# RMS-norm row factors moved behind the products in a two-layer decoder trunk

## The chip, the cores and the metric

The kernel runs on one core of one Trainium2 chip. The metric is the device time of one execution, in microseconds (us). A profile of one execution, taken by the hardware profiler, shows what each engine did: TensorE (PE, with its weight loads PEld), VectorE (DVE), ScalarE (ACT), GpSimd (POOL) and SyncE (SP), which issues the DMAs.

## The reference

Two layers of a decoder trunk over 256 rows of 1024 numbers, all float32. What matters here is where the norms stand:

```
def rms_norm(x, g):
    y = x * rsqrt(mean(x * x, axis=-1) + EPS)
    return y * g

for i in range(2):
    h = rms_norm(x, attn_norm_g[i])
    x = x + mixer_i(h)                        # layer 0: attention; layer 1: gMLP + convolution
    x = x + swiglu(rms_norm(x, ffn_norm_g[i]))

def swiglu(h):  g, u = split(h @ w_in);  return (silu(g) * u) @ w_out
```

The factor `rsqrt(mean(x * x) + EPS)` is one number per row, so it commutes with a product over the columns; the gain `g` is one number per column. In layer 1 the mixer projects `h` to four parts (`gu`, `gv`, `ca`, `cg`) and adds a bias to each before a gelu or a sigmoid; `ca * sigmoid(cg)` goes through a causal convolution of 31 taps.

## The kernel before

The 256 rows are two tiles of 128 (m = 0, 1); the 1024 columns are eight blocks of 128, or two halves of 512 (n = 0, 1). `xs` holds the residual by rows in SBUF. Each float32 product is made of three passes of TensorE (`passes`, L223 to L228): operands are split into a rounded high part and the remainder. For the weights, `Block.split_hi` (L133, ScalarE) and `Block.split_lo` (L137, VectorE, for some blocks GpSimd) do that. The steps lie in a queue `todo`; `tick` and `pump` take them out as products are written down, `Block.at` takes out what a product needs at once, and `held` stops `tick`. Weights come in blocks of 1 MB (L116) into three raw buffers.

Where one stage ends and the next begins, `close` (L372 to L411) does the norm. It happens three times: **site 0** (attention to the first feed-forward), **site 1** (first feed-forward to layer 1's mixer) and **site 2** (mixer to the second feed-forward). At each:

1. The last eight steps of the output product of m = 0 (`tail_steps`) run, and `residual` (L358, VectorE) adds the result to `xs`; `square` (L302, ScalarE) sums the squares.
2. `row_factor` (L307, L308 on VectorE, a power on GpSimd at L310) makes the factor, `norm_rows` (L331, VectorE) multiplies `xs` by the factor and by the gain, which `gain_rows` (L321) has loaded as 128 equal rows.
3. `norm_T` transposes the normed rows on TensorE (L340, four 128x128 per half), and `split` (L239 on ScalarE, L240 on VectorE) writes high part and remainder into `xT`, the moving or stationary operand of the next stage.
4. For m = 0 this is laced into the eight steps of m = 1's tail (`N_T0`); for m = 1 it is laced into the first product of the next stage by `follow` (`N_T1`). `SPLITS` says how many weight steps are taken out in between.

TensorE's order is that of the program text. In `close`, VectorE and GpSimd run in text order too (`in_order`); elsewhere the scheduler chooses.

`FeedForward.first_steps` (L426 to L438) makes the first 256 columns row-wise; `rest` (L447 to L483) makes the others transposed: two sums of 128x512 per j, silu (L468), product (L470), split. In layer 1, `gv_steps` (L1017 to L1023) is row-wise; `gated` (L1091 to L1107) makes `cg` and `ca` transposed into one bank, takes the sigmoid (L1100, ScalarE) and the product (L1101, VectorE) into `cpad`. The taps of three of the four channel tiles run on VectorE (L1075, L1077, 93 in all); those of the fourth run on TensorE and are read out at L1064. Then `mean` (L1172, TensorE) starts the layer norm of the convolution, whose chain goes back and forth between the engines up to the last rows of the output product.

Of the kernel before, what the change touches and what calls it, by code (L numbers as in the profile page):

```python
# [60 lines left out]
SPLITS = ((2, 3, 7), (12, 3, 1), (7, 3, 5))  # L61
N_T0 = (5, 4, 5)
N_T1 = (10, 5, 10)
# [9 lines left out]
def trunk_kernel(ctx: ExitStack, tc: tile.TileContext, a: dict, out: bass.AP):  # L73
# [168 lines left out]
    def in_order(*engines):  # L242
# [12 lines left out]
        ("attn_g", a["attn_norm_g"][0].rearrange("(k p) -> k p", p=P)),  # L255
# [13 lines left out]
    assert nvec <= 64  # L269
    vec = consts.tile([P, 64], F32, name="vec")  # L270

    def load_vecs(names):
        vec_rows = scratch()[:64, :P]
        for name, src in vec_src:
            if name in names:
                nc.sync.dma_start(vec_rows[rows[name]:rows[name] + src.shape[0], :], src)
        return vec_rows

# [7 lines left out]
    nc.gpsimd.memset(neg_half, -0.5)  # L286
    mask = consts.tile([P, S], F32, name="mask")
# [4 lines left out]
    vec_rows = load_vecs(("attn_g",))  # L292
# [11 lines left out]
    def row_factor(ss):  # L304
# [4 lines left out]
        r = small.tile([P, 1], F32, name="rm")  # L309
        nc.gpsimd.tensor_tensor(r, t[:, 1:2], neg_half[:, :1], op=ALU.pow)  # L310
        return r

# [22 lines left out]
    def norm_T(m, n, xn, xT, ptag):  # L335

        pt = ptag()
        ms = slice(m * P, (m + 1) * P)
        for j in range(4):
            nc.tensor.transpose(pt[:, j * P:(j + 1) * P], xn[n][:, j * P:(j + 1) * P], ident)  # L340
        split(xT[0][:, 4 * n:4 * n + 4, ms], xT[1][:, 4 * n:4 * n + 4, ms], pt.rearrange("p (a b) -> p a b", b=P))
# [14 lines left out]
    def residual(m, n, pss):  # L356
        ns = slice(n * 512, (n + 1) * 512)
        nc.vector.tensor_tensor(xs[:, m, ns], pss[m][n], xs[:, m, ns], op=ALU.add)  # L358
# [13 lines left out]
    def close(site, lhs, ws, k0, pss, gB, ptag, tail0=True):  # L372
# [3 lines left out]
        ss = [small.tile([P, 2], F32, name="ss") for _ in range(MT)]  # L376

        def end(m, n):
            residual(m, n, pss)
            square(m, n, ss[m])  # L380

# [29 lines left out]
        return xT, follow  # L411


    class FeedForward:
        def __init__(self, layer, fp, ptag):
            self.layer = layer
# [9 lines left out]
        def first_steps(self, xT, m):  # L426
# [9 lines left out]
            nc.scalar.activation(sg[:, :256], ps[:, :256], AF.Silu)  # L436
# [10 lines left out]
        def rest(self, xT, extra=iter(()), cut_last=False):  # L447
# [852 lines left out]
```

## Time and profile before

| what | value |
|---|---|
| median of 3 runs | 631.66 us (630.54 to 631.96) |
| the profiled execution | 633.2 us |
| its span, first to last instruction | 631.4 us |
| mean granted clock of TensorE in it | 0.989 of full speed |
| TensorE busy | 609.0 us, 96% of the span |
| VectorE / ScalarE / GpSimd busy | 67% / 55% / 19% |
| read from HBM | 102.69 MB, 164 GB/s over the span |

How to read it: TensorE is busy almost all the time, so a microsecond is won only where TensorE waits, runs at the lower of its clock levels (1.2 instead of 2.4 GHz), or has work taken away. A row of a timeline gives start, duration, engine, line, operation and shapes, and in brackets how long the engine was idle before it and who released it. Matmul records overlap, since their ends are modelled; the time between two starts is the better measure.

### The profile page before, as it was taken

What the parts mean: (1) busy time and instruction counts of PE and PEld (TensorE: products, weight loads), DVE (VectorE), ACT (ScalarE), POOL (GpSimd) and SP (SyncE); (2) the same over time, 40 slices, a digit from 0 to 9 for tenths busy, and PEclk for the clock granted to TensorE, in tenths of its full rate; (3) what the DMA queues carried; (4) which work ended last, traced back from release to release, by engine and by line L of the source; (5) the groups of instructions that cost most, each with busy time, mean ns of one, the idle gap of its engine ahead of it and who ended that gap; (6) DMA issues with size and microseconds to landing.
All of it is one profiled execution on the core that took longest, in us unless ns stands there. A gap on an engine that the chain in (4) does not pass through costs nothing.

```text
span 631.4 us, 8906 instructions
## 1 busy us (share of the span) xinstructions
PE 609.0 (96%) x3420; PEld 517.6 (82%) x3420; DVE 421.1 (67%) x710; ACT 345.7 (55%) x621; POOL 121.7 (19%) x97
## 2 busy tenths in 40 slices
PE   7989799999999999999998999988999999999997
PEld 5867577787988888888886899867988888888886
DVE  3799998547666648664446389986766666665431
ACT  5764686555655587553446775446455555554320
POOL 1998321101000000000003695550000000000000
PEclk9999799999999999999999799999999999999999
DMA  7855424224766437555552553225656555555401
GB/s 248 308 196 175 158 106 132 70 66 149 245 225 215 146 128 266 185 168 185 199 197 67 167 199 134 68 89 178 208 193 201 196 174 173 193 199 190 145 0 67
DMA packets 72791, 104.32 MB, mean 165 GB/s; under 512 B 3068, under 2 KB 56492, under 8 KB 72748
## 3 DMA queue, kind: packets, MB, share of 16 engines
q1 hardware_dynamic: 72748, 103.74, 49.5%
q8 instruction: 27, 0.44, 0.3%
q14 instruction: 16, 0.13, 0.1%
HBM read 102.69 MB, written 1.05 MB: 164 GB/s over the span
## 4 chain that ended last, share of the span: by engine, by line
PE 52%; issue 29%; DVE 11%; POOL 3%; ACT 2%; DMA 1%; SPq 1%; POOLq 0%; DVEq 0%; ACTq 0%
PE mm L233 15%; PE mm L225 8%; PE mm L227 8%; PE mm L234 8%; PE mm L226 8%; DVE wlo L137 3%; DVE scr L331 2%; PE tq L700 1%; DMA raw<-in_even_w_in 1%; POOL rm L310 1%; DVE t L627 1%; PE po L728 1%; ACT whi L133 1%; DVE t L621 1%; PE tq L718 1%
## 5 line engine op out<-in xcount | busy, mean ns | idle before, releaser
L133 ACT ACTIVATE whi<-raw 128x1024 fp32r<-128x1024 f32 (+1 forms) x192 | 197.7, 1040 | 175.7 <-PE mm L233 80.1
L137 DVE TENSOR_TENSOR wlo<-raw,whi 128x1024 fp32r<-128x1024 f32 (+1 forms) x166 | 206.3, 1248 | 124.5 <-ACT whi L133 122.9
L233 PE MATMUL mm<-xT,whi 128*128 128x512 f32 x640 | 226.8, 399 | 0.0
L234 PE MATMUL mm<-xT,wlo 128*128 128x256 f32 x640 | 179.7, 281 | 0.0
L233 PEld LDWEIGHTS mm<-xT,whi 128*128 128x128 f32 x640 | 120.2, 188 | 29.6 <-issue 0.2
L234 PEld LDWEIGHTS mm<-xT,wlo 128*128 128x128 f32 x640 | 120.9, 189 | 0.0
L225 PE MATMUL mm<-whi,xT 128*128 128x512 f32 (+1 forms) x176 | 68.2, 387 | 0.6 <-ACT xT L545 0.5
L137 POOL TENSOR_TENSOR wlo<-raw,whi 128x1024 fp32r<-128x1024 f32 (+1 forms) x26 | 62.9, 2439 | 19.7 <-ACT whi L133 19.6
L227 PE MATMUL mm<-whi,hT_lo 128*128 128x512 f32 (+1 forms) x176 | 66.5, 378 | 0.0
L226 PE MATMUL mm<-wlo,hT_hi 128*128 128x512 f32 (+1 forms) x176 | 66.5, 378 | 0.0
L225 PE MATMUL mm<-whi,hT_hi 128*128 128x512 f32 (+1 forms) x176 | 66.4, 378 | 0.0
L227 PE MATMUL mm<-whi,xT 128*128 128x512 f32 (+1 forms) x176 | 64.1, 364 | 1.1 <-DVE xT L240 1.1
L226 PE MATMUL mm<-wlo,xT 128*128 128x512 f32 (+1 forms) x176 | 64.3, 366 | 0.5 <-DVE wlo L137 0.5
L310 POOL TENSOR_TENSOR rm<-st,neg_half 128x1 f32<-128x1 f32 x8 | 7.1, 894 | 188.9 <-DVE st L308 188.9
L225 PEld LDWEIGHTS mm<-whi,xT 128*128 128x128 f32 x176 | 34.5, 196 | 7.8 <-issue 1.6
L227 PEld LDWEIGHTS mm<-whi,xT 128*128 128x128 f32 x176 | 34.6, 196 | 6.8 <-DVE xT L240 1.8
L226 PEld LDWEIGHTS mm<-wlo,xT 128*128 128x128 f32 x176 | 34.7, 197 | 4.8 <-DVE wlo L137 1.3
L225 PEld LDWEIGHTS mm<-whi,hT_hi 128*128 128x128 f32 x176 | 33.1, 188 | 6.4
L226 PEld LDWEIGHTS mm<-wlo,hT_hi 128*128 128x128 f32 x176 | 33.1, 188 | 6.4
L227 PEld LDWEIGHTS mm<-whi,hT_lo 128*128 128x128 f32 x176 | 33.0, 188 | 6.4
L464 DVE TENSOR_TENSOR scr<-mm,scr 128x256 f32<-128x256 f32 x80 | 33.2, 418 | 5.8 <-ACT scr L463 5.7
L1077 DVE SCALAR_TENSOR_TENSOR cv<-cpad,cw,cv 128x256 f32<-128x256 f32 x87 | 35.7, 481 | 0.2
(226 smaller groups left out, 868.6 us busy)
## 6 DMA issues: line engine op xcount, KB each, us to landing
raw<-in_ffn_w_in SPq DMA_DIRECT2D x44, 1024.0 KB
raw<-in_ffn_w_out SPq DMA_DIRECT2D x22, 1024.0 KB
raw<-in_even_w_in SPq DMA_DIRECT2D x10, 1024.0 KB
raw<-in_odd_w_in SPq DMA_DIRECT2D x8, 1024.0 KB
raw<-in_even_w_out SPq DMA_DIRECT2D x4, 1024.0 KB
raw<-in_odd_w_out SPq DMA_DIRECT2D x4, 1024.0 KB
xs<-in_x SPq DMA_DIRECT2D x4, 256.0 KB
raw<-in_even_w_in SPq DMA_DIRECT2D x4, 256.0 KB
```

The costliest lines, as they stand in the source:

```text
L133: nc.scalar.activation(self.half(f)[0][:, r], self.source(f)[:, r], AF.Copy)
L137: self.lo_engine.tensor_tensor(lo[:, r], self.source(f)[:, r], hi[:, r].bitcast(F32), op=ALU.subtract)
L225: nc.tensor.matmul(ps, lhs[0], rhs[0], start=first, stop=False)
L226: nc.tensor.matmul(ps, lhs[0], rhs[1], start=False, stop=False)
L227: nc.tensor.matmul(ps, lhs[1], rhs[0], start=False, stop=last)
L233: nc.tensor.matmul(bank, w[0], x[2][:, k, :, :].rearrange("p a b -> p (a b)"), start=k == 0, stop=False)
L234: nc.tensor.matmul(bank[:, :S], w[1], x[0][:, k, :], start=False, stop=k == KT - 1)
L310: nc.gpsimd.tensor_tensor(r, t[:, 1:2], neg_half[:, :1], op=ALU.pow)
L331: nc.vector.scalar_tensor_tensor(xn[n], xs[:, m, n * 512:(n + 1) * 512], r, gB[:, n * 512:(n + 1) * 512], op0=ALU.mult, op1=ALU.mult)
L464: nc.vector.tensor_tensor(s, bank[:, :S], s, op=ALU.add)
L621: nc.vector.scalar_tensor_tensor(t1v, psv, rx[m], c, op0=ALU.mult, op1=ALU.mult)
L1077: nc.vector.scalar_tensor_tensor(conv[:, ct, :] if t == TAPS - 1 else acc, cpad[:, ct, t:t + S], cw[:, t, ct:ct + 1], acc, op0=ALU.mult, o ...
```

## The change

The row factor is no longer applied before the transposition. `close` transposes the raw residual as soon as it is added, and the gain is applied, as a column of factors, while high part and remainder are taken out of PSUM. The factor is computed later and applied behind the products: as the scale of the first silu, as a factor of the residual addition, and as a row of factors (`factor_rows`) that multiplies transposed results.

```diff
-SPLITS = ((2, 3, 7), (12, 3, 1), (7, 3, 5))
-N_T0 = (5, 4, 5)
-N_T1 = (10, 5, 10)
+N_T0 = ((1, 3), (1, 3), (1, 3))
+REST = (4, 4, 4)
+N_T1 = ((1, 4), (1, 2), (1, 4))
...
+    def factor_rows(r, ptag):
+
+        pb = ptag()
+        for m in range(MT):
+            dg = scratch()[:, :P]
+            nc.vector.tensor_scalar(dg, ident, r[m], None, op0=ALU.mult)
+            nc.tensor.matmul(pb[:, m * P:(m + 1) * P], ones, dg, start=True, stop=True)
+        rB = act.tile([P, S], F32, name="rB", tag="rB")
+        nc.scalar.activation(rB, pb[:, :S], AF.Copy)
+        return rB[:, None, :].to_broadcast([P, 2, S])
...
-    def gain_rows(src):
-        g = act.tile([P, D], F32, name="gB", tag="gB", bufs=1)
-        nc.sync.dma_start(g, bcast(src))
-        return g
-
-    def norm_rows(m, ss, gB, splits):
-
-        r = row_factor(ss)
-        pump(splits)
-        xn = []
-        for n in range(2):
-            xn.append(scratch())
-            nc.vector.scalar_tensor_tensor(xn[n], xs[:, m, n * 512:(n + 1) * 512], r, gB[:, n * 512:(n + 1) * 512],
-                                           op0=ALU.mult, op1=ALU.mult)
-        return xn
...
+    def x_T(m, n, ptag):
         pt = ptag()
+        for j in range(4):
+            nc.tensor.transpose(pt[:, j * P:(j + 1) * P], xs[:, m, (4 * n + j) * P:(4 * n + j + 1) * P], ident)
+        return pt
+
+    def x_split(m, n, pt, gain, xT, js=range(4)):
+
         ms = slice(m * P, (m + 1) * P)
...
+        for j in js:
+            nc.scalar.activation(xT[0][:, 4 * n + j, ms], pt[:, j * P:(j + 1) * P], AF.Copy, scale=col(gain, 4 * n + j))
+        for j in js:
+            k = 4 * n + j
+            nc.vector.scalar_tensor_tensor(xT[1][:, k, ms], pt[:, j * P:(j + 1) * P], col(gain, k),
+                                           xT[0][:, k, ms].bitcast(F32), op0=ALU.mult, op1=ALU.subtract)
...
+            nc.vector.scalar_tensor_tensor(xs[:, m, ns], pss[m][n], r[m], xs[:, m, ns], op0=ALU.mult, op1=ALU.add)
...
-        held[0] = True
         region = in_order("DVE", "Pool")
         end(0, 1)
-        xn0 = norm_rows(0, ss[0], gB, SPLITS[site][0])
         for i, (n, k) in enumerate(tail_steps(lhs, ws, k0, 1, pss, BY_BLOCK)):
+            if i == REST[site]:
+                held[0] = True
             if i == 3 and ws[0].index + 4 < len(plan):
                 plan[ws[0].index + 4].ahead()
-            if i == N_T0[site]:
-                norm_T(0, 0, xn0, xT, ptag)
-                pump(SPLITS[site][1])
+            if i in N_T0[site]:
+                turn(0, N_T0[site].index(i), ptag)
             if k == 3:
                 end(1, n)
-        norm_T(0, 1, xn0, xT, ptag)
-        xn1 = norm_rows(1, ss[1], gB, SPLITS[site][2])
+        rs.append(row_factor(ss[0]))
 
         def follow(steps, ptag):
 
             for i, _ in enumerate(steps):
-                if 0 <= i - N_T1[site] < 2:
-                    norm_T(1, i - N_T1[site], xn1, xT, ptag)
-            held[0] = False
+                if i in N_T1[site]:
+                    turn(1, N_T1[site].index(i), ptag)
+                    if i == N_T1[site][1]:
+                        rs.append(row_factor(ss[1]))
+                        held[0] = False
             region.close()
...
-            nc.scalar.activation(sg[:, :256], ps[:, :256], AF.Silu)
+            nc.scalar.activation(sg[:, :256], ps[:, :256], AF.Silu, scale=self.r[m])
...
+                if i == 9:
+                    rB = factor_rows(self.r, self.ptag)
...
-                sg = scratch()
-                nc.scalar.activation(sg, sums[0], AF.Silu)
+                sg = sums[0]
+                sgv = sg.rearrange("p (a b) -> p a b", b=S)
+                nc.gpsimd.tensor_tensor(sgv, sgv, rB, op=ALU.mult)
+                nc.scalar.activation(sg, sg, AF.Silu)
...
-            nc.vector.tensor_tensor(gn[:, m, :], ps, bv, op=ALU.add)
+            nc.vector.scalar_tensor_tensor(gn[:, m, :], ps, r[m], bv, op0=ALU.mult, op1=ALU.add)
...
         follow(gv_steps(0), spare)
+        rB = factor_rows(r, spare)
+
+        def scaled(ps):
+            t = scratch()
+            nc.vector.tensor_tensor(t.rearrange("p (a b) -> p a b", b=S), ps.rearrange("p (a b) -> p a b", b=S), rB, op=ALU.mult)
+            return t
...
-                    sigmoid = nc.scalar.activation(sgm, ps[:, :S], AF.Sigmoid, bias=col("b_in", 12 + ct))
-                    nc.vector.scalar_tensor_tensor(cpad[:, ct, TAPS - 1:], ps[:, S:], col("b_in", 8 + ct), sgm,
+                    t = scaled(ps)
+                    sigmoid = nc.scalar.activation(sgm, t[:, :S], AF.Sigmoid, bias=col("b_in", 12 + ct))
+                    nc.vector.scalar_tensor_tensor(cpad[:, ct, TAPS - 1:], t[:, S:], col("b_in", 8 + ct), sgm,
                                                    op0=ALU.add, op1=ALU.mult)
...
+            t = scaled(pu)
             for f in range(2):
-                gelu = nc.scalar.activation(guT[:, 2 * j + f, :], pu[:, f * S:(f + 1) * S], AF.Gelu_apprx_tanh,
+                gelu = nc.scalar.activation(guT[:, 2 * j + f, :], t[:, f * S:(f + 1) * S], AF.Gelu_apprx_tanh,
                                             bias=col("b_in", 2 * j + f))
```

The rest is bookkeeping: the four gains are loaded as columns with the other vectors (site 0's by a load and a transposition of eight rows during attention), the three loads of 512 KB by `gain_rows` go, the helpers that layer 0's start had for itself are now shared, `r` is handed on from `close`, and the tile of ones is made at the start.

## Rows read from the trace of the kernel before

**Rows 1.** Busy times by stretch, feed-forward 0: stretch, length, busy of PE, PEld, DVE, ACT, POOL, PEclk, DMA.
```profile
256.00:272.00 16.00, 16.00 (x92) 13.88 (x91) 10.43 (x16) 8.87 (x14) 0.00 (x0) 1.00 0.53 179
```

**Rows 2.** Timeline of TensorE at site 0.
```profile
146.36 0.40 PE L227 MATMUL mm<-whi,cT_lo 128*128 128x512 f32 x1
146.87 0.33 PE L340 MATMUL tq<-ident,scr 128*128 128x128 f32 x1
...
151.03 0.28 PE L226 MATMUL mm<-wlo,xT 128*128 128x256 f32 x1
151.87 0.39 PE L227 MATMUL mm<-whi,xT 128*128 128x256 f32 x1 [0.56 <-DVE xT L240]
...
154.00 0.28 PE L226 MATMUL mm<-wlo,xT 128*128 128x256 f32 x1
154.12 0.28 PE L227 MATMUL mm<-whi,xT 128*128 128x256 f32 x1
154.91 0.30 PE L340 MATMUL tq<-ident,scr 128*128 128x128 f32 x1 [0.50 <-DVE scr L331]
```

**Rows 3.** Waits at site 2 (432 to 447 us): total, times, longest.
```profile
PE tq L340 <- DVE scr L331: 0.5, 1, 0.5
PE mm L227 <- DVE xT L240: 0.5, 1, 0.5
```

**Rows 4.** Busy times by stretch, site 1 (columns as in rows 1).
```profile
333.63:340.47 6.84, 6.71 (x33) 5.04 (x32) 5.14 (x6) 4.35 (x6) 3.15 (x3) 1.00 0.28 96
...
344.88:347.80 2.92, 0.17 (x2) 0.03 (x1) 2.92 (x2) 1.47 (x6) 2.92 (x2) 0.96 0.00 0
347.80:354.38 6.58, 6.27 (x23) 5.16 (x24) 4.56 (x4) 3.93 (x12) 4.85 (x2) 0.50 0.39 111
```

**Rows 5.** Timeline of VectorE and GpSimd: sites 0 and 1, and a later norm.
```profile
146.06 1.41 DVE L331 SCALAR_TENSOR_TENSOR scr<-xs,rm,gB 128x512 f32<-128x512 f32 x2 [0.45 <-POOL rm L310]
...
336.39 3.62 DVE L331 SCALAR_TENSOR_TENSOR scr<-xs,rm,gB 128x512 f32<-128x512 f32 x2 [0.67 <-POOL rm L310]
337.06 2.40 POOL L137 TENSOR_TENSOR wlo<-raw,whi 128x1024 fp32r<-128x1024 f32 x1 [0.71 <-ACT whi L133]
...
419.06 2.41 DVE L1192 TENSOR_SCALAR scr<-ident,cvr 128x128 f32<-128x128 f32 x1 [0.66 <-POOL cvr L299]
```

**Rows 6.** Instructions of single lines: ns min/median/max, first and last start.
```profile
L545 ACT ACTIVATE xT<-tq,vec x16: 350/378/432, 5.9 to 17.2; 128x128 fp32r<-128x128 f32 x16
L548 DVE SCALAR_TENSOR_TENSOR xT<-tq,vec,xT x16: 334/340/351, 6.7 to 18.8; 128x128 fp32r<-128x128 f32 x16
L310 POOL TENSOR_TENSOR rm<-st,neg_half x8: 548/553/1469, 26.9 to 442.0; 128x1 f32<-128x1 f32 x8
L1023 DVE TENSOR_TENSOR gn<-mm,bv x2: 692/692/692, 352.9 to 370.6; 128x512 f32<-128x512 f32 x2
L1197 PE MATMUL cv<-scr,ones x4: 275/316/377, 418.1 to 422.3; 128*128 128x128 f32 x4
```

**Rows 7.** Layer 1's taps: VectorE's stretch (columns as in rows 1).
```profile
362.19:411.05 48.86, 48.17 (x378) 45.50 (x377) 45.38 (x109) 27.38 (x46) 33.31 (x24) 1.00 0.38 130
```

**Rows 8.** Timeline at both ends of that stretch, ScalarE, VectorE, TensorE.
```profile
360.38 1.28 ACT L1100 ACT_TABLE_LOAD   x1
...
362.19 0.48 DVE L1101 SCALAR_TENSOR_TENSOR cpad<-mm,vec,scr 128x256 f32<-128x256 f32 x1 [8.59 <-ACT scr L1100]
...
408.61 0.48 DVE L1064 TENSOR_SCALAR conv<-mm,vec 128x256 f32<-128x256 f32 x1 [0.67 <-PE mm L227]
410.47 0.81 PE L1172 MATMUL tq<-conv,ones 128*128 128x256 f32 x3
```

**Rows 9.** Two other stalls of TensorE: stretches (columns as in rows 1) and timeline.
```profile
63.38:67.14 3.76, 0.16 (x2) 0.00 (x1) 3.69 (x5) 1.58 (x4) 3.30 (x2) 1.00 0.58 234
67.14:74.30 7.16, 7.16 (x25) 5.61 (x26) 7.12 (x29) 5.02 (x17) 1.64 (x1) 0.54 0.39 146
...
427.20 0.50 PE L227 MATMUL mm<-whi,oT_lo 128*128 128x512 f32 x1 [1.93 <-DVE oT_lo L240]
```

More of the change, by code (lines that the diff above doesn't have):

```diff
@@ L268, in trunk_kernel, with load_vecs, vecs_T @@
     nvec = at
[L269 to L273, printed above, removed]
+    assert nvec <= P
+    vec = consts.tile([P, nvec], F32, name="vec")
+    def load_vecs(first, last, vec_rows=None):
+        vec_rows, r0 = scratch()[:, :P] if vec_rows is None else vec_rows, rows[first]
         for name, src in vec_src:
-            if name in names:
-                nc.sync.dma_start(vec_rows[rows[name]:rows[name] + src.shape[0], :], src)
-        return vec_rows
+            if rows[first] <= rows[name] <= rows[last]:
+                nc.sync.dma_start(vec_rows[rows[name] - r0:rows[name] - r0 + src.shape[0], :], src)
+        return vec_rows
+    def vecs_T(vec_rows, first, n, ptag):
+        pt = ptag()
+        nc.tensor.transpose(pt[:, :n], vec_rows[:n, :], ident[:n, :n])
+        nc.vector.tensor_copy(vec[:, rows[first]:rows[first] + n], pt[:, :n])
     def col(name, i):
@@ L370, in trunk_kernel, with close, turn @@
     BY_BLOCK = [(n, k) for k0 in (0, 2) for n in range(2) for k in (k0, k0 + 1)]
-    def close(site, lhs, ws, k0, pss, gB, ptag, tail0=True):
+    def close(site, lhs, ws, k0, pss, r, gain, ptag, tail0=True):
         xT = new_xT()
         ss = [small.tile([P, 2], F32, name="ss") for _ in range(MT)]
+        rs = []
         def end(m, n):
-            residual(m, n, pss)
+            residual(m, n, pss, r)
             square(m, n, ss[m])
+        def turn(m, n, ptag):
+            x_split(m, n, x_T(m, n, ptag), gain, xT)
         if tail0:
@@ L500, in trunk_kernel @@
         warm(WARM[0])
-        pt = tq()
-        nc.tensor.transpose(pt[:, :8], vec_rows[:8, :], ident[:8, :8])
-        nc.vector.tensor_copy(vec[:, :8], pt[:, :8])
+        vecs_T(vec_rows, "attn_g0", 8, tq)
         w_dk = [blocks["dk", h] for h in range(2)]
@@ L534, in trunk_kernel, with first_T, first_split @@
         pts = {}
-        def x_T(m, n):
-            pts[m, n] = pt = tq()
-            for j in range(4):
-                nc.tensor.transpose(pt[:, j * P:(j + 1) * P], xs[:, m, (4 * n + j) * P:(4 * n + j + 1) * P], ident)
-        def x_split(m, n, js=range(4)):
-            ms = slice(m * P, (m + 1) * P)
-            pt = pts[m, n]
-            for j in js:
-                nc.scalar.activation(xT[0][:, 4 * n + j, ms], pt[:, j * P:(j + 1) * P], AF.Copy, scale=col("attn_g", 4 * n + j))
-            for j in js:
-                k = 4 * n + j
-                nc.vector.scalar_tensor_tensor(xT[1][:, k, ms], pt[:, j * P:(j + 1) * P], col("attn_g", k),
-                                               xT[0][:, k, ms].bitcast(F32), op0=ALU.mult, op1=ALU.subtract)
+        def first_T(m, n):
+            pts[m, n] = x_T(m, n, tq)
+        def first_split(m, n, js=range(4)):
+            x_split(m, n, pts[m, n], "attn_g0", xT, js)
         ps_dk = [mm_bank() for _ in range(MT)]
@@ L912, in trunk_kernel @@
         run_units(units, filler)
-        xT, follow = close(0, cT, ws_b, 4, pss, gB, tq, tail0=False)
+        xT, r, follow = close(0, cT, ws_b, 4, pss, None, "ffn_g0", tq, tail0=False)
     mid = ExitStack()
@@ L931, in odd_setup @@
     def odd_setup(ptag):
-        vec_rows = load_vecs([n for n, _ in vec_src])
+        vec_rows = load_vecs("attn_g1", vec_src[-1][0])
         nc.sync.dma_start(bv, bcast(a["odd_b_in"][0, 512:1024]))
-        nc.gpsimd.memset(ones, 1.0)
         def load_ws(g0):
@@ L951, in odd_setup @@
         yield
-        pt = ptag()
-        nc.tensor.transpose(pt[:, :nvec], vec_rows[:nvec, :], ident[:nvec, :nvec])
-        nc.vector.tensor_copy(vec[:, 8:nvec], pt[:, 8:nvec])
+        vecs_T(vec_rows, "attn_g1", nvec - rows["attn_g1"], ptag)
         ws_T(ws0, 0)
@@ L1234, in trunk_kernel @@
         ws = [blocks["oo", k0] for k0 in (4, 6)]
-        xT, follow = close(2, cT, ws, 4, pss, gB, spare)
+        xT, r, follow = close(2, cT, ws, 4, pss, None, "ffn_g1", spare)
     mid.close()
```

61 lines of the change are left out of this document (31 added, 30 removed).

## The prediction

> **What bounds the kernel now.** I read the busy times by stretch first. In the feed-forwards TensorE is full, 16.00 of 16 us, beside a VectorE with 10.43 [rows 1]; nothing is to be won there except work taken off TensorE, and the change takes none off. So I looked for stretches in which TensorE waits or runs at its lower clock, with the list of waits, and then read the three norms in the timeline.
>
> Site 0: starts of 256-wide passes lie 0.12 us apart (154.00 to 154.12), yet 151.03 is followed by 151.87 and 154.12 by 154.91 [rows 2]: 0.72 and 0.67 lost, the first to the remainder of the second half of m = 0, the second to the normed rows of m = 1. Ahead of them 146.36 to 146.87 loses 0.28 (512-wide passes lie 0.23 apart). With a small one of 0.2 that is 1.9 us. Site 2 shows the same two waits, 0.5 each by their modelled ends [rows 3], so 0.7 each by starts as above, and the small one: 1.6.
>
> Site 1 is the dear one. The eight steps of m = 1's tail take 6.84 us [rows 4]; 24 passes at 0.226 and two groups of transpositions at 0.36 are 6.15. Then TensorE waits 2.92 us for the normed rows of m = 1, and comes back at a granted clock of 0.50 (1.2 GHz) for 6.58 us [rows 4], in which it does about 3.1 us of work. Why is the norm late? VectorE's two L331 take 1.41 us at site 0 and 3.62 us at site 1, where GpSimd starts a weight remainder of 2.40 at 337.06 [rows 5]: a VectorE instruction with both tensors in SBUF waits until GpSimd's is over. All together, site 1 loses 0.7 + 0.3 + 2.9 + 0.3 + 3.1 = 7.3 us.
>
> **The change part by part.**
>
> *Transposing the raw residual.* At each site the statistics, the power and L331 (twelve in all) leave TensorE's path. What is late next? The transpositions need only the addition, and of m = 0's two additions the later ends before step 1 of the tail, its place being step 3. For m = 1 the last addition ends some 0.9 us after the tail, and its transpositions stand two steps or more later. The split behind each grows: four 128x128 on ScalarE and four on VectorE, 0.38 and 0.34 each [rows 6], some 1.1 us a side when they overlap, instead of 0.6 and 0.7. For m = 0 half 1 it starts after step 3 and has four steps of 0.7 until the next stage begins: covered, by about 1 us; uncovered it costs 0.5 to 1 a site. So all of 1.9 + 1.6 goes: **-3.5**.
>
> *Weight steps.* `SPLITS` goes, and ticks run until step 4. Counted by hand, the first two feed-forward blocks are fully split before the tail of m = 1 ends at sites 0 and 2, and both `gv` blocks at site 1; what `REST` stops is for blocks used 5 us and more later. Nothing; bounds 0 and 1.2 (one remainder) a site.
>
> *Row of factors*, three times: two small products on TensorE. Their kind takes 0.32 a record and two records each [rows 6], overlapping, 0.23 a product by starts: 3 x 0.46 = **+1.4**, between 0.5 (one product each hidden in a wait) and 2. In the feed-forwards nine steps lie between factor and use, so nothing waits. Site 0's column of gains costs one transposition, 0.1.
>
> *Site 1 on TensorE.* Without stalls: tail until 333.63 + 6.15 = 339.8, eight steps of 0.69 and two transpositions until 346.0. Then the row of factors waits. The last transposition is done at 342.6; split by 344.3, statistics 0.4, power 0.55 [rows 6]: factor at 345.4. Right behind, in GpSimd's order, stand three weight remainders, so the small VectorE product on `ident` should do what L1192 did at 419.06, 2.41 us [rows 5]: 347.9. Queued behind that product on VectorE is only `gn`, which nobody awaits soon. TensorE waits 2.0 (bounds: 0, if GpSimd is not yet on; 4.9, if both diagonals are caught) and is done at 348.5, where it is now at 352.67 and 0.7 slow after that. **-4.7** up to here, without a drop of the clock.
>
> *Layer 1 on VectorE.* The question is whether these 4.7 last. From the first gate product at 362.19 to the last tap at 411.05 VectorE is busy 45.38 of 48.86 [rows 7], and TensorE comes to `mean` at 410.47, 0.6 before the last tap ends [rows 8]: both bound. The change adds six 128x512 multiplications out of PSUM, 0.69 each by L1023 [rows 6]. TensorE will finish the first gate at 354.5; multiplication, table load 1.28 [rows 8] and sigmoid put the product at 357, or up to 359.4 if GpSimd is on, since the product now reads two SBUF tensors. I take 358, 4.2 earlier. From there 48.86 + 5 x 0.69 (3.5) + waits of the three later gate products on GpSimd (between 0 and 2.4 each; GpSimd is on for half and more of this stretch, so the middle, 3.6) - idle time filled (0 to 3.5; VectorE now lags, so 3.0) = 411.0. Shift of the last tap: **-0.1**, bounds -4.7 and +4. So what site 1 wins, VectorE takes: 0 in place of -4.7. The row of factors there costs nothing then: +0.9 instead of +1.4.
>
> *A new stall.* TensorE would wait for L1064, which ends 2.0 before the last tap [rows 8], from 405.8 to 408.9: 3.1 us. Stalls of 2.92 [rows 4] and 3.76 [rows 9] were followed by 6.6 and 7.2 us near the lower clock; one of about 2.1 before 427.20 was not. The lower clock then falls on `mean` and the four steps behind it, beside VectorE's chain: 0 to 2.7, **+0.7** since most lies beside the chain.
>
> *Silu's factor on GpSimd*, twenty of 128x512, half a weight remainder of 2.40: 1.2 us each. It delays VectorE's SBUF work by as much per 11.5 us, which has 5.6 of 16 free [rows 1]; `hT` is needed only after the last j. Behind the waiting silu on ScalarE stand the copies that free TensorE's banks; a bank takes 2.9 us to fill and there are four. Nothing; without that cover 1.2 once per feed-forward. Factors inside residual, silu and `gn` replace an operand of instructions that are there. The loads of gain rows were on no path; on SyncE one small load of eight rows takes the place of a 512 KB one ahead of weight loads that wait for buffers anyway.
>
> Sum: -3.5 + 0.9 + 0.1 - 0.1 + 0.7 = -1.9, against the profiled execution's 633.2 (span 631.4), which is 1.5 above the median. On the median 631.66 that gives **629.8 us**; with its own bounds 628.3 to 631.5.
>
> **The rivals.**
>
> *The gain gets through.* VectorE's additions fit into its 3.5 us of idle time, the gate products meet GpSimd in gaps, and the scheduler puts taps where it waited. Then the last tap keeps up with TensorE: -3.5 + 1.5 - 4.7 = -6.7, no stall, 625.0. For it: the idle time is there. Against it: 3.5 us of multiplications fill it alone.
>
> *Slower: the gate products wait for GpSimd.* L1101 now reads PSUM and takes 0.48 [rows 8]; afterwards both its tensors lie in SBUF. If each of three meets a full remainder, 7.2 in place of 3.6, and the idle time doesn't shrink as much, 1.5 in place of 3.0, the last tap comes 5 us later, and the stall grows and brings the lower clock for certain: -1.9 + 5.0 = +3.1, 634.8; at half that surplus, about 632.3. It decides from a last tap 2 us later than now. The Trainium skill, page "GPSIMD Engine Reference", section "8. Key points", says the same of the SBUF interfaces: GpSimd shares them with VectorE, and contends with VectorE instructions of two SBUF inputs. By that rule all four gate products are exposed, 634.8 at worst; without it the sum would have 0 in place of 3.6 and come to 626.2. The trace agrees with the rule for L331.
>
> *The split becomes the wait.* If eight small instructions a half come later than the old two, sites 0 and 2 keep their stalls: -1.9 + 3.5 = +1.6, 633.3. Against it is the cover of 1 us.
>
> **How the numbers follow.** Forecast 0.47, gain gets through 0.22, gate products wait 0.21, split waits 0.10. About 0.2% (1.26 us) is what a measurement of this kernel can tell from no change. Of the forecast's 0.47, centred 0.6 beyond that bound, 0.29 is faster and 0.17 same; of the second all but 0.01 faster; of the third 0.16 slower, 0.05 same; of the fourth half and half. Faster 0.50, same 0.28, slower 0.22. The range leaves out half of the second and half of the third: 624.8 to 634.0.
>
> **What would show it.** Right: no wait on L331's successors at any site; granted clock 1.00 over 340 to 354; a wait of about 2 us for the diagonals ahead of the first gate; the gate products longer than 0.5 us; VectorE without gaps up to the last tap, at about the same distance from site 0 as now, and TensorE waiting some 3 us ahead of `mean`. Wrong: the last tap several us earlier (gain through) or later (slower), half clock at the row of factors, or waits on the small splits.

## The result: slower by 2.8%, and the profile after

The changed kernel takes 648.88 us (median of 4 runs, 646.61 to 652.45) beside 631.58 for the kernel before: ratio 1.0282, 95% interval 1.0228 to 1.0335. Forecast were 629.8 us and a range up to 634.0. The profiled execution is one of 646.61 us with a span of 644.9, 13.5 more than before.

To find where the 13.5 us come from I cut the span at one instruction that every version has, the residual addition of the second half of m = 0 at each site (its start on VectorE in the timeline). The stretches of all versions of this study, from their profiled executions, in us:

| kernel | start to site 0 | site 0 to 1 | site 1 to 2 | site 2 to end |
|---|---|---|---|---|
| before | 142.6 | 191.2 | 98.7 | 198.9 |
| after | 147.8 | 194.8 | 102.2 | 200.1 |
| e1 gain late | 141.9 | 193.3 | 102.5 | 200.1 |
| e2 hold longer | 147.7 | 191.3 | 104.4 | 196.1 |
| e3 no gu factor | 150.4 | 194.0 | 99.3 | 200.1 |
| e4 all three | 142.3 | 191.3 | 100.1 | 196.1 |
| e5 gu order | 150.7 | 194.8 | 104.2 | 198.6 |
| e6 vec 80 | 150.0 | 194.4 | 103.3 | 199.9 |
| e7 all kept | 141.9 | 191.3 | 105.3 | 196.1 |
| e8 diagonals on ScalarE | 140.0 | 191.3 | 104.9 | 196.1 |
| e9 steps run | 140.3 | 191.3 | 106.7 | 196.1 |
| e10 rows first at site 1 | 139.9 | 190.4 | 98.3 | 196.2 |
| e11 before, site 1 clear | 141.1 | 190.4 | 94.9 | 198.9 |
| e12 sites 0 and 2, site 1 clear | 141.0 | 191.3 | 94.7 | 196.1 |

After loses 5.2, 3.5, 3.5 and 1.2: all four stretches are longer, the attention too, in which the change has only one transposition of a column of gains. (The first stretch can't be read closer than some 3 us: the five versions with the changed kernel's attention lie at 147.7 to 150.7, mean 149.3, and the nine without its late load at 139.9 to 142.6, mean 141.2, which is 8.1 between the groups.) The list of waits of TensorE in the changed kernel begins with these (total us, times, longest):

```profile
PE tq L286 <- DMA ffn_rows<-in_ffn_norm_g: 10.4, 1, 10.4
PE tq L469 <- DVE scr L462: 4.5, 2, 2.3
PE cv L331 <- DVE scr L330: 2.6, 1, 2.6
PE tq L1151 <- ACT scr L1155: 2.6, 1, 2.6
PE tq L1196 <- DVE conv L1099: 2.0, 1, 2.0
```

The waits of [rows 3] and the stall of 2.92 [rows 4] are gone; there is no wait for normed rows or their split at any site. In their place stand these five; the fourth was 0.7 before, the other four are new. The first one in the timeline, of the SyncE queue and of TensorE:

```profile
27.21 0.25 SPq L693 DMA_DIRECT2D sub_rows<-in_diff_subln_g  x1
34.16 2.60 SPq L117 DMA_DIRECT2D raw<-in_even_w_in  x2
36.81 0.39 SPq L281 DMA_DIRECT2D ffn_rows<-in_ffn_norm_g  x1
...
31.81 0.39 PE L228 MATMUL mm<-whi,xT 128*128 128x512 f32 x1
42.63 0.27 PE L286 MATMUL tq<-ident,ffn_rows 8*128 8x8 f32 x1 [10.44 <-DMA ffn_rows<-in_ffn_norm_g]
```

SyncE issues in order. The load of eight rows of gains stands behind two weight loads that are not issued until 34.16, when their buffer is free. So it is issued at 36.81, and the transposition, which stands in TensorE's order ahead of the dv products, waits 10.44 us for it. Only the first 4.6 us of that are the wait for the issue (36.81). The other 5.4 us, from the end of the issue to the landing, pass while the two weight loads ahead of it move; the DMA share is 0.91 or more in each us from 36 to 41. VectorE works on meanwhile and the stall of 3.76 [rows 9] does not come again; 5.2 us are left at site 0 in this execution.

The second wait, behind site 0: the timeline of VectorE and TensorE, and busy times by stretch (columns as in rows 1, with GB/s last):

```profile
160.24 4.62 DVE L138 TENSOR_TENSOR wlo<-raw,whi 128x1024 fp32r<-128x1024 f32 x4
164.77 0.42 DVE L462 TENSOR_TENSOR scr<-mm,scr 128x256 f32<-128x256 f32 x1
...
165.25 0.44 PE L469 MATMUL tq<-ident,scr 128*128 128x128 f32 x2 [2.18 <-DVE scr L462]
...
162.00:164.00 2.00, 1.07 (x9) 0.86 (x8) 2.00 (x3) 1.69 (x3) 0.00 (x0) 1.00 0.09 17
166.00:168.00 2.00, 2.00 (x12) 2.00 (x11) 1.05 (x2) 1.17 (x2) 0.00 (x0) 0.50 1.09 359
```

Weight steps start again at step 4, as soon as the norm's last transposition is issued, and four remainders of the weights come onto VectorE ahead of the first product of gate and up (L462). It ends 165.2, TensorE waits 2.18 us for it and then works at 0.50, which is 1.2 GHz. Site 2 has the same wait of 2.3 and the same clock.

Site 1, GpSimd, VectorE and TensorE:

```profile
355.24 0.55 POOL L322 TENSOR_TENSOR rm<-st,neg_half 128x1 f32<-128x1 f32 x1 [4.30 <-DVE st L320]
355.76 9.46 POOL L138 TENSOR_TENSOR wlo<-raw,whi 128x1024 fp32r<-128x1024 f32 x4
...
356.12 2.06 DVE L330 TENSOR_SCALAR scr<-ident,rm 128x128 f32<-128x128 f32 x1
...
358.24 0.49 PE L331 MATMUL cv<-scr,ones 128*128 128x128 f32 x2 [2.60 <-DVE scr L330]
```

This is the forecast wait for the diagonal: 2.6 where 2.0 was said. The clock stays at 1.00 behind it. The gated products begin 15.9 us behind site 1's addition instead of 18.8, and the first gate product comes 26.2 behind it instead of 28.4. But the last tap ends 81.0 us behind it instead of 77.2. The odd stage, VectorE, ScalarE and TensorE, and the stretch of the taps:

```profile
368.76 0.92 DVE L1124 SCALAR_TENSOR_TENSOR cpad<-scr,vec 128x256 f32<-128x256 f32 x1 [3.48 <-ACT scr L1123]
373.78 1.65 DVE L1124 SCALAR_TENSOR_TENSOR cpad<-scr,vec 128x256 f32<-128x256 f32 x1
...
399.40 2.52 DVE L1054 TENSOR_SCALAR gn<-gn,mv__3786,gvr 128x512 f32<-128x512 f32 x1
401.84 3.22 DVE L1099 SCALAR_TENSOR_TENSOR cv<-cpad,cw,cv 128x256 f32<-128x256 f32 x8
404.98 0.68 DVE L1068 TENSOR_TENSOR scr<-mm,rB 128x512 f32<-128x512 f32 x1
...
406.61 1.28 ACT L1180 ACT_TABLE_LOAD   x1
408.52 1.12 PE L1151 MATMUL tq<-wsT,gn 128*64 128x128 f32 x8 [2.56 <-ACT scr L1155]
418.34 0.48 DVE L1086 TENSOR_SCALAR conv<-mm,vec 128x256 f32<-128x256 f32 x1 [4.46 <-PE mm L228]
...
368.76:423.52 54.76, 50.24 (x368) 46.68 (x367) 49.81 (x114) 28.01 (x46) 34.62 (x25) 0.94 0.35 116
```

The gate products take 0.92, 1.65, 0.47 and 0.82 instead of 0.48 each. The factor of the second gu product (L1068 at 404.98) stands behind a norm that runs beside GpSimd (2.52 where the same norm of m = 0 takes 0.55; the kernel before has this too, 2.51) and eight taps; behind it stand gelu, a table load and the scaling that frees the spatial products' bank, and TensorE waits 2.56 for that and then works at 0.50 over 408 to 414. VectorE in its turn waits 4.46 for TensorE's taps, with 12 of its own taps standing behind this read-out; before it was 0.67 [rows 8], with five. Against [rows 7] its busy time grows by 4.4 us and its idle time by 1.5: this one wait grows by 3.8, all other idle time shrinks by 2.3.

### The profile page after: what moved, and what is told of

Same layout as the page of the kernel before. It is cut to its first block, busy times and chain, and to the rows that moved or that the text cites. A ratio compares the mean times of both kernels' runs of the same rounds, so it can differ in the third digit from the quotient of the medians.

```text
span 644.9 us, 9078 instructions
## 1 busy us (share of the span) xinstructions
PE 610.0 (95%) x3433; PEld 520.8 (81%) x3433; DVE 422.4 (65%) x747; ACT 354.9 (55%) x660; POOL 147.1 (23%) x117
## 3 DMA queue, kind: packets, MB, share of 16 engines
HBM read 101.12 MB, written 1.05 MB: 158 GB/s over the span
## 4 chain that ended last, share of the span: by engine, by line
PE 69%; DVE 16%; POOL 5%; issue 3%; ACT 3%; DMA 2%; SPq 1%; POOLq 0%; ACTq 0%; DVEq 0%
PE mm L234 23%; PE mm L235 12%; PE mm L226 9%; PE mm L228 9%; PE mm L227 9%; DVE cv L1099 4%; DVE wlo L138 3%; POOL rsh L638 2%; PE tq L720 1%; PE po L748 1%; ACT whi L134 1%; DMA raw<-in_even_w_in 1%; DMA raw<-in_odd_w_in 1%; ACT xT L353 1%; PE tq L738 1%
## 5 line engine op out<-in xcount | busy, mean ns | idle before, releaser
L234 PE MATMUL mm<-xT,whi 128*128 128x512 f32 x640 | 224.3, 395 | 0.0
L496 POOL TENSOR_TENSOR scr<-scr,rB 128x512 f32<-128x512 f32 x20 | 26.8, 1340 | 206.6 <-DVE scr L491 176.3
L226 PEld LDWEIGHTS mm<-whi,xT 128*128 128x128 f32 x176 | 35.3, 201 | 6.7 <-issue 1.5
L228 PEld LDWEIGHTS mm<-whi,xT 128*128 128x128 f32 x176 | 35.2, 200 | 4.9
```

The lines of the kernel that those rows point to most:

```text
L226: nc.tensor.matmul(ps, lhs[0], rhs[0], start=first, stop=False)
L228: nc.tensor.matmul(ps, lhs[1], rhs[0], start=False, stop=last)
L234: nc.tensor.matmul(bank, w[0], x[2][:, k, :, :].rearrange("p a b -> p (a b)"), start=k == 0, stop=False)
L496: nc.gpsimd.tensor_tensor(sgv, sgv, rB, op=ALU.mult)
```

## The experiments

Times are medians; each ratio is to the kernel before, run on the same chip. The changed kernel's own ratio is 1.0282.

**e1.** The transposition of the column of gains is moved, nothing else:

```diff
         run(projections(("dq",)))
-        vecs_T(ffn_rows, "ffn_g0", 8, tq)
...
         run(projections(("dv",)))
+        vecs_T(ffn_rows, "ffn_g0", 8, tq)
```

> The changed kernel, with one edit: the transposition of site 0's column of gains stands behind the dv projection instead of ahead of it, so that TensorE no longer waits 10.4 us for its small load, which SyncE issues behind weight loads. Theory: the wait and the half clock behind it are what the attention stage lost (its end is 5.2 us later than before the change, since VectorE caught up with 5 us of its own backlog meanwhile), so this gives 5 us: about 643 to 645 against 648.9. Rival: VectorE bounds the attention stage anyway and the wait is cover for it: under 1.5 us.

Measured: 640.61 us, ratio 1.0152 (1.0109 to 1.0194). The wait is gone, site 0 comes after 141.9 us. That is 1.3% or some 8 us (by the two intervals some 4 either way), more than the 5.2 read at site 0 in one execution; it agrees with the 8.1 between the two groups of the table, and the stretch to site 1 is 1.5 shorter too. The wait behind site 0 is there as before, but not the lower clock behind it (see the last section).

**e2.** Weight steps stay stopped until the first product of the next stage is over:

```diff
                     if i == N_T1[site][1]:
                         rs.append(row_factor(ss[1]))
-                        held[0] = False
+            held[0] = False
             region.close()
```

> The changed kernel, with one edit: weight steps are held until the end of the first product of the next stage, as before the change, and not only until the second transposition of m = 1. Theory: the 2.2 us waits of TensorE for the first hidden half at both feed-forwards, and the half clock behind them, come from four weight remainders of 1.2 us that stand on VectorE right ahead of the product behind the silu; spread into earlier gaps they leave it alone: both waits under 0.7 us, 4 to 7 us less, 642 to 645. Rival: VectorE has that much to do there in any order, and the product stays late: under 1.5 us.

Measured: 643.11 us, ratio 1.0194 (1.0156 to 1.0232), 0.9% or 5.5 us, again with some 4 either way. The wait behind site 0 is 0.2 and behind site 2 gone; the two feed-forward stretches are 3.5 and 4.0 shorter. At site 1 the same edit does harm (+2.1): GpSimd in e2,

```profile
343.05 4.78 POOL L138 TENSOR_TENSOR wlo<-raw,whi 128x1024 fp32r<-128x1024 f32 x2 [61.91 <-ACT whi L134]
...
347.94 4.72 POOL L138 TENSOR_TENSOR wlo<-raw,whi 128x1024 fp32r<-128x1024 f32 x2
352.63 0.54 POOL L322 TENSOR_TENSOR rm<-st,neg_half 128x1 f32<-128x1 f32 x1
```

the power of m = 0 now comes behind four remainders (behind one in the changed kernel), and TensorE waits 2.7 and 1.6 us for the two diagonals. The program text up to this power is the same in both kernels: stopping the weight steps in the text did not keep the scheduler from placing remainders ahead of a norm's power.

**e3.** The row factor of gu is left out (the gated branch's factors, gn's and the feed-forwards' are kept):

```diff
-            t = scaled(pu)
             for f in range(2):
-                gelu = nc.scalar.activation(guT[:, 2 * j + f, :], t[:, f * S:(f + 1) * S], AF.Gelu_apprx_tanh,
+                gelu = nc.scalar.activation(guT[:, 2 * j + f, :], pu[:, f * S:(f + 1) * S], AF.Gelu_apprx_tanh,
```

> The changed kernel without the row factor of the gu projection (left out, with its two multiplications on VectorE). Theory (order): the second multiplication stands on VectorE behind a blocked normalisation and eight taps, so gelu, the table load behind it and the read-out of the spatial product come late, TensorE waits 2.6 us and runs at half clock, and its own taps end late, for which VectorE then waits 4.5 us: without it the last tap comes 4 to 7 us earlier, 642 to 645. Rival (amount, as the prediction had it): only the 2 x 0.7 us of VectorE's work go, 1.4 us, 647.5.

Measured: 641.73 us, ratio 1.0177 (1.013 to 1.0224): by the medians 1.05% or 6.6 us, for two instructions of 0.68. In the profiled execution the odd stretch is 2.9 us shorter, the wait of TensorE for the scaling 0.7 and the last tap 76.5 us behind site 1. With intervals of half a per cent on either ratio the difference of the medians is good to some 4.5 us: more than the rival's 1.4, and the profiled execution's 2.9 lies below the theory's 4 to 7. The size stays open.

**e4.** e1, e2 and e3 together (gu's row factor is left out here too).

> The three edits together (gu's row factor is left out). If the three causes are independent and all of them, the sum of the three gains, 13 to 19 us: 630 to 636, that is at the time before the change or a little under it. If they hide one another, clearly less than the sum.

Measured: 631.71 us, ratio 1.0029 (1.0006 to 1.0051). The three gains alone add up to 3.2%, together they are 2.5%: additive within the noise, since each gain is good to some 0.7%. e2's harm at site 1 is in the sum and in e4 alike (waits of 2.7 and 1.8 us, and half clock behind them). So the three causes hold most of the loss. But with them gone, and a piece of the work left out, the change is where the kernel before was; what it should have won is still missing.

**e5.** The order around the second gu product:

```diff
+        def tap():
+            with tc.issue_after(gu_scaled[0]) if gu_scaled[0] is not None else ExitStack():
+                tap_dve()
...
-                    tap_dve()
+                    tap()
...
+        credit[0] -= 3
+        held[0] = True
         last = project_gu(1)
+        held[0] = False
```

> The changed kernel with nothing left out; only the order around the second gu product is different: the weight steps stop while its passes are issued, three taps fewer are put on VectorE ahead of its row factor, and the taps that come later may not pass it. Theory (the 7 us that leaving gu's row factor out brought are order, not amount: the factor is held up by a GpSimd remainder and eight taps, behind it gelu, the table load, the scaling that frees the spatial products, and TensorE, which then loses its clock): the factor starts at about 403 instead of 404.98, the TensorE wait of 2.56 us on that scaling falls below 1, no half clock over 408 to 415, time 642 to 645.5. Rival (VectorE has too much to do; the two multiplications themselves are what costs): VectorE's work is the same, the last tap ends within 1 us of 423.5, time 647 to 650.

Measured: 651.32 us, ratio 1.0318 (1.0268 to 1.0368). The theory's steps are there (the factor comes as soon as its product is done, 60.5 us behind site 1 instead of 62.4; TensorE waits 0.8 for the scaling and keeps full clock over 408 to 416; the last tap ends 77.6 us behind site 1 instead of 81.0), and the time is not. VectorE behind the last tap:

```profile
423.08 4.56 DVE L138 TENSOR_TENSOR wlo<-raw,whi 128x1024 fp32r<-128x1024 f32 x2
427.56 0.68 DVE L1210 SCALAR_TENSOR_TENSOR scr<-tq,conv 128x512 f32<-128x512 f32 x1
```

The weight steps that were pushed back come out ahead of the mean's subtraction, where TensorE waits 3.9 us for it; from the last tap to site 2 it is 26.6 us instead of 21.3.

**e6.** Only the tile of per-row constants is wider, which moves every later tile by 32 bytes:

```diff
-    vec = consts.tile([P, nvec], F32, name="vec")
+    vec = consts.tile([P, 80], F32, name="vec")
```

> The changed kernel, with the tile of per-row constants 80 columns wide instead of 68: nothing else. It moves every tile behind it in SBUF up by 32 bytes, which puts the halves of the weights at the same offset within 64 bytes as before the change. In the changed kernel the 512-wide passes of the first feed-forward's output come every 0.234 us, where before they came every 0.227, and the first products of the second feed-forward every 0.347 a pair, where before it was 0.353. Theory (where tiles lie sets the pace of passes): the paces change by 1 to 3 percent in at least one of the feed-forwards, the time by between -2 and +2 us. Rival (the pace comes from the order of work or from what else reads SBUF): paces as in the changed kernel, time 647 to 650.

Measured: 648.17 us, ratio 1.0264 (1.0205 to 1.0323): as the changed kernel, and the paces are as there (last section). The theory falls.

**e7** is e1, e2 for sites 0 and 2 only, and e5, so that everything is computed; **e8** is e7 with the diagonals on ScalarE; **e9** is e7 without stopping the weight steps at gu and with `credit[0] -= 5`.

```diff
-                        held[0] = False
+                        held[0] = site != 1
+            held[0] = False
             region.close()
...
-            nc.vector.tensor_scalar(dg, ident, r[m], None, op0=ALU.mult)
+            nc.scalar.activation(dg, ident, AF.Copy, scale=r[m])
```

> The change with nothing left out, and three moves: the column of gains is transposed behind the dv products, weight steps stay stopped at sites 0 and 2 until the norm's steps are over (at site 1 as in the changed kernel), and the second gu product's factor has its place ahead of three taps and of the weight steps. Theory (three separate orderings cost the time): 630 to 634, no wait over 1 us behind site 0 or site 2, TensorE's wait for the diagonal at site 1 2 to 3 us as in the changed kernel. Rival (VectorE's amount of work sets the odd stage): 634 to 638, with the last tap some 3 us later against site 1 than in the run that leaves the gu factor out.

> As the run with the three moves, and the factors' diagonals are made by ScalarE (identity times the row factor as its scale) instead of VectorE. Theory (at site 1 the small VectorE product waits for a GpSimd remainder, 2.06 instead of 0.29 us): TensorE's wait at site 1 falls from 2.6 to about 1 us, the first gated products begin 1.5 to 2 us earlier, time 1 to 2 us below the run with the three moves. Rival (ScalarE is in other work there, twelve diagonals of the taps in a row, 3.6 us): the wait is as long, time the same or above.

> As the run with the three moves, nothing left out, but the weight steps are no longer stopped around the second gu product; five taps fewer are put ahead of its factor instead of three. Theory (in the run with the three moves the weight steps that were pushed behind the taps cost some 5 us between the last tap and site 2, 26 us there instead of 21): 632 to 635, from the last tap to the residual of site 2 about 21.5 us. Rival (that stretch is longer for another reason): 635 to 638, still 25 to 26 us.

Measured: e7 636.51 us, ratio 1.0089 (1.0063 to 1.0115); e8 635.37, 1.0071 (1.0047 to 1.0095); e9 638.47, 1.0106 (1.0076 to 1.0136). All three lie above the kernel before. e7 came out as its rival had it: 634 to 638 us, and the last tap, 79.1 us behind site 1, 2.7 later than in e3, which leaves gu's factor out; the stretch from site 1 to 2 is 105.3. In e8 TensorE's wait for the diagonal is 0.7 and the gated products begin 1.9 us earlier, as its theory said, yet the first gate product on VectorE comes no earlier (26.3 us behind site 1's addition, 26.4 in e7): it now waits 5.5 us for ScalarE's sigmoid, which stands behind a weight split that waits 3.24 us for its load. The 1.1 us between the medians of e7 and e8 are not clear of noise. In e9 the stretch behind the last tap is 22.3 us, as that theory said, but the last tap is later (84.4 behind site 1), because the norm beside GpSimd took 2.52 again and two weight remainders came ahead of the factor. Against the changed kernel's 102.2 us between sites 1 and 2, the three orders tried (e5, e7, e9) are 2.0, 3.1 and 4.5 longer: each frees the place it aims at and is charged at another. That it is the order and not the amount is therefore not shown; whether an order exists that has room for the two multiplications stays open.

**e11.** The question left was the prediction's own: does the odd stage eat whatever site 1 wins? Read again, the stall of [rows 4] belongs to m = 1's own two L331, not to the 3.62 us of [rows 5], which are m = 0's. VectorE and GpSimd in the kernel before:

```profile
344.83 5.59 DVE L331 SCALAR_TENSOR_TENSOR scr<-xs,rm,gB 128x512 f32<-128x512 f32 x2 [0.74 <-POOL rm L310]
...
344.76 7.89 POOL L137 TENSOR_TENSOR wlo<-raw,whi 128x1024 fp32r<-128x1024 f32 x3
```

The edit: the kernel before, with GpSimd's remainders ordered behind the normed rows of m = 1 at site 1:

```diff
-            step(f)
+            with tc.issue_after(barrier[0]) if barrier[0] and step == b.split_lo and b.lo_engine is nc.gpsimd else ExitStack():
+                step(f)
...
-        xn1 = norm_rows(1, ss[1], gB, SPLITS[site][2])
+        xn1 = norm_rows(1, ss[1], gB, 0 if site == 1 else SPLITS[site][2])
+        if site == 1:
+            behind = small.tile([P, 2], F32, name="st2")
+            barrier[0] = nc.gpsimd.tensor_copy(behind[:, 0:1], xn1[1][:, 511:512]).ins
+            pump(SPLITS[site][2])
```

> The kernel before, with one edit: at site 1 GpSimd's weight remainders are ordered behind a one-column copy that needs the normed rows of m = 1, so that none runs beside VectorE's two L331 there (5.59 us together, 1.41 at site 0). Theory (that is what made the stall of 2.92 us and the lower clock behind it): the stall falls below 1 us, granted clock 1.00 over the steps behind it, the gated products start 3 to 5 us earlier. Whether the end keeps it: if taps on VectorE bound the odd stage (as the prediction had it), the last tap moves less than 1 us and the time stays within 630 to 632; if not, 626 to 629.

Measured: 625.51 us, ratio 0.9914 (0.9885 to 0.9943). VectorE and TensorE at site 1, the clock behind it, and the stretch of the taps:

```profile
342.50 1.41 DVE L333 SCALAR_TENSOR_TENSOR scr<-xs,rm,gB 128x512 f32<-128x512 f32 x2 [0.74 <-POOL rm L312]
343.40 0.63 PE L342 MATMUL cv<-ident,scr 128*128 128x128 f32 x4 [0.69 <-DVE scr L333]
...
344.00:346.00 2.00, 2.00 (x14) 1.69 (x13) 0.86 (x2) 1.95 (x7) 1.94 (x2) 1.00 0.40 152
...
357.26:403.32 46.06, 45.37 (x354) 42.70 (x354) 45.13 (x109) 27.15 (x46) 33.34 (x24) 1.00 0.40 138
```

The two multiplications take 1.41 instead of 5.59, the wait is 0.69, the clock stays at 1.00, the gated products begin 14.2 us behind site 1's addition (18.8 before). And the end keeps most of it: VectorE is busy as long as in [rows 7], 45.13, but its idle time falls from 3.48 to 0.93, the last tap ends 71.8 us behind site 1 instead of 77.2, and the stretch from site 1 to 2 is 3.8 shorter.

**e10** and **e12** keep the change at sites 0 and 2 alone, with e1's edit and, at these two sites, e2's. At site 1 the rows are multiplied by their factor ahead of the transposition (e10 on ScalarE, with GpSimd's remainders ordered behind the power of m = 1; e12 on VectorE with e11's order), so the odd stage has no added factor; the transpositions there come some steps later. From e10:

```diff
+        if site == 1:
+            xn[1] = scaled_rows(1, row_factor(ss[1]))
...
-            t = scaled(pu)
+            t = pu
```

> The change at sites 0 and 2 only, nothing left out. At site 1 the rows are multiplied by their factor before they are transposed, by ScalarE, with the gains in the split as in the change; so gates, gu and gn need no factor and no row of factors is made there; GpSimd's weight remainders are ordered behind the power of m = 1. Column of gains and weight steps at sites 0 and 2 as in the run with the three moves. Theory (site 1's stall came from VectorE's multiplications waiting for GpSimd, and without the six added multiplications VectorE can keep what is won): TensorE waits under 1.5 us at site 1, no half clock, first gate product 24 to 26 us behind the residual of site 1 instead of 28.4, last tap as much earlier, time 625 to 629. Rival (taps bound the odd stage whatever site 1 does): last tap 77 us behind the residual of site 1 as before, 629 to 632.

> The change at sites 0 and 2 only, nothing left out, with the edit of the run before at site 1: there VectorE multiplies the rows by their factor before they are transposed, as in the kernel before (the gains go into the split), and GpSimd's weight remainders are ordered behind a one-column copy that needs the rows of m = 1. Column of gains and weight steps as in the run with the three moves. Theory (site 1's win of some 5.5 us holds because no factor is added in the odd stage; sites 0 and 2 give 3.5 less 0.9 for two rows of factors, of which some 1 is lost to slower passes in the first feed-forward's output): 622 to 625.5. Rival (the change has nothing to give at sites 0 and 2 once site 1 is clear): 625.5 to 628.

Measured: e10 626.58 us, ratio 0.993 (0.9905 to 0.9956); e12 625.35, 0.9916 (0.9886 to 0.9947). Both beat both kernels. e10 still waits 1.9 us at site 1, with half clock behind it, and keeps 3.4 of the last tap's 5.4. e12 is as fast as e11, no more. So the gain over the kernel before is e11's edit; what the change itself gives at sites 0 and 2 is below what these runs can tell (some 0.4%, or 2.7 us). Between e7 and e12 only site 1 and e5's order differ, and the stretch from site 1 to 2 is 10.7 us shorter in e12.

## Why the prediction was wrong, point by point

- **"Site 0's column of gains costs one transposition, 0.1"** is the step that failed first: some 8 us by e1. The text had the small load "ahead of weight loads that wait for buffers"; two of them stand ahead of it in the queue and on the DMA engines, and TensorE needs it at once, where the 512 KB load it replaced was needed only at the norm. I priced the instruction and not its due time on a queue that is served in order.
- **"Weight steps. Nothing; bounds 0 and 1.2 a site"** failed: 3.5 and 4.0 in the feed-forward stretches by e2, the lower clock behind the waits included. The count looked at whether the blocks would be split in time. It did not ask what stands in VectorE's order when the steps start again: four remainders of 1.15 ahead of the first gate product.
- **"Layer 1 on VectorE"** failed in its sizes and in its conclusion. The first gate product was to come 4.2 us earlier and came 2.2 earlier. Of the 2.0 missing, 1.3 are TensorE's: it has the first gate done 22.0 us behind site 1's addition, not 20.7 (354.5 less 333.83). The rest is ScalarE's, whose sigmoid stands behind a weight split that waits 1.17 us for its load. The stretch from there to the last tap was to grow by 4.1 (3.5 + 3.6 - 3.0) and grew by 5.9, so the last tap is 3.8 later instead of 0.1 earlier. Of the terms, the multiplications were right (0.68 each), the waits of the three later gate products were 1.5 instead of 3.6 (1.65 + 0.47 + 0.82, less three of 0.48; the first adds 0.4), and "idle time filled, 3.0" had the wrong sign: 2.3 us of the old idle time were filled, but 3.8 came at the read-out of TensorE's taps, so it grew by 1.5. Six multiplications were priced as time on VectorE; what waits for each was not asked. Behind gu's second one stand ScalarE, the bank and TensorE, and in the end VectorE waits for TensorE. e3 gives more than the 1.4 us of gu's two multiplications themselves: 2.9 in the profiled stretch, 6.6 by the medians. No run moves the read-out behind the 12 taps, which would have filled that wait; what it would give is open.
- **"A new stall"** had the engines the wrong way round: it had TensorE wait 3.1 us for the read-out of its taps and then lose its clock beside `mean`. Instead VectorE waits 4.46 at this read-out, and TensorE waits 2.0 at `mean` for the last taps; the granted clock behind that is 1.00 over 422 to 426. So the lower clock of the +0.7 did not come there; it came behind the scaling that frees the bank, for which no term stood.
- **"What site 1 wins, VectorE takes"** was right in sign for the change itself: with the factors the win of site 1 is gone at the last tap. The reason, that VectorE's busy time binds the stage as it is, is refuted by e11: without added factors most of the win goes through, as VectorE's idle time in the stretch falls from 3.48 to 0.93. The reading ahead of it was wrong too: the 3.62 us given as the reason for the late norm are m = 0's, and the stall belongs to m = 1's 5.59.
- **The rival of GpSimd** (634.8) was true in kind: three of the four gate products took longer, one of them 1.65. The Trainium skill (page "GPSIMD Engine Reference", section "8. Key points") names two kinds of VectorE instructions that contend with GpSimd for the SBUF interfaces: those with two SBUF inputs, and those in a 2-port mode. The runs agree with the first kind for L1124 (1.65); L330 (2.06 instead of 0.29) and L1054 (2.52 instead of 0.55), with one tensor and a column as inputs, are slowed as well, and no run here shows whether they are of the second kind. The rival's place in the sum was small beside what was missing from the sum altogether.
- **Right**: no stall on normed rows or splits at any site; full clock over site 1; the wait for the diagonal, 2.6 for 2.0, its cause included; the feed-forward's silu factor on GpSimd is hidden (TensorE is busy 60.00 of 60 us beside six of them, last section). With e2's edit and the other pace of passes of the last section taken out (+1.7 - 0.6 in feed-forward 0, -2.0 in 1), sites 0 and 2 gave by an estimate 191.3 - 191.2 - 1.1 = -1.0 and 196.1 - 198.9 + 2.0 = -0.8, where -1.4 and -1.1 stood in the sum. These are good to about 1 us: e11, whose program is the kernel before's from site 0 to 1, has 190.4 there instead of 191.2.

The forecast's bound for the last tap (+4) held the odd stage's 3.8. But none of its cases has a load that comes late or a remainder ahead of the first product, so no rival could have reached 648.9.

## What to carry to other kernels

A load is priced by when its reader needs it and by what waits in its queue ahead of it, not by its size; a reader on the critical engine turns a late small load into a stall. When work is freed from a hold, ask which instruction of the next stage it will stand in front of. And before work is moved off a stalled path, test the cheaper edit: here the stall at site 1 was two VectorE instructions beside GpSimd's weight remainders, and putting these behind them gave 0.9% where the whole rewrite lost 2.8%.

## What was not expected of the hardware

**The same stall, two clocks.** The wait behind site 0 is 2.18 us in the changed kernel and in e1, behind the same instructions. In the changed kernel the stretch 166 to 168 has the clock at 0.50; in e1 the stretch that answers to it:

```profile
159.36 0.44 PE L469 MATMUL tq<-ident,scr 128*128 128x128 f32 x2 [2.18 <-DVE scr L462]
...
160.00:162.00 2.00, 2.00 (x19) 2.00 (x18) 1.52 (x3) 1.57 (x3) 0.00 (x0) 1.00 1.09 358
```

Of the waits shown above, 2.60 at site 1 is followed by 1.00 and 2.56 at the spatial products by 0.50. So a wait of 2 to 3 us may or may not cost the clock, and its price can't be told from its length. The Trainium skill, page "TensorE: Matmul & The Clock Gate", section "Part 1: The HAM clock gate", has the chip decide at moments that are not tied to the kernel's own; the pair agrees with that, though nothing here shows the moments.

**The pace of passes differs by versions.** Busy times in the output of feed-forward 0 (30 us) and in the gates of feed-forward 1 (60 us), TensorE full in all of them; the counts are the point. The kernel before:

```profile
292.00:322.00 30.00, 30.00 (x134) 24.86 (x133) 12.86 (x11) 11.02 (x11) 0.00 (x0) 1.00 0.54 181
482.00:542.00 60.00, 60.00 (x342) 52.05 (x341) 39.31 (x53) 33.81 (x54) 0.00 (x0) 1.00 0.56 181
```

The changed kernel:

```profile
299.00:329.00 30.00, 30.00 (x130) 24.11 (x128) 13.20 (x11) 10.61 (x10) 0.00 (x0) 1.00 0.54 175
495.00:555.00 60.00, 60.00 (x348) 52.91 (x348) 41.34 (x55) 34.42 (x55) 6.80 (x6) 1.00 0.59 192
```

134 against 130 passes, and 342 against 348, in the same order and at the same granted clock: 3% slower over some 55 us (1.7), 1.8% faster over some 113 us (2.0); the gates of feed-forward 0 are some 0.6 faster (357 against 355 in 60 us). e11 keeps the counts of before (134 and 342), e12 those of after (130 and 349), e6 those of after (129 and 348) although its tiles lie 32 bytes further. What sets the pace stays open; the difference is of the size of what the change was to win.

**GpSimd slows down as well.** In the kernel before, both powers of one column at site 0 (144.56 and 152.50) took 1.47 us instead of 0.55 [rows 6], each beside a weight remainder of 1.22 that VectorE had begun 0.16 us earlier.
